# Hybrid pooling and short-convolution block, fp32 on one core: plain transfers issued by SP instead of GpSimd, joins spread over ticks, and eight more Strassen steps

## The chip, the core and the metric

The kernel runs on one core of a Trainium2 chip. Times are device microseconds. Before the change the median of 3 runs is 2392.21 us (2391.22 to 2397.08).

A core has a matrix engine (PE, with weight loads shown as PEld), VectorE (DVE), ScalarE (ACT) and GpSimd (POOL). SP computes nothing and issues transfers. POOL issues transfers too, among its own work; those that add to what stands at the destination (called gathers or joins here) are all POOL's.

## The reference

For 256 tokens of 4096 channels, all float32:

```python
h = rmsnorm(x, norm_w)
u_p, z_p, u_c, b_c, c_c, z_c, g_logit = split(h @ w_in)   # four times 2048 and two, then 2 * 4096 columns
y_pool = causal_multiscale_pool(u_p, pool_w, pool_scale) * silu(z_p)
y_conv = b_c * (conv_b + causal width-3 convolution of (c_c * u_c)) * silu(z_c)
br = einsum('bsnc,ncd->bsnd', stack([y_pool, y_conv]), w_branch)
gates = sigmoid(g_logit + gate_b)
x = x + sum(gates * br, over n) @ w_out
return rmsnorm(x, final_norm_w)
```

The pooling averages each channel group over a trailing window of 2, 4, 8 or 16 tokens, subtracts the token and applies a 512 x 512 map for each group. The weights, some 580 MB, are read once.

## The kernel before, in words

**Products.** Every float32 operand is split into a high part rounded to fp32r and the low rest, and a product is three matmuls (high x high, high x low, low x high) of 128 x 128 by 128 x 512. The work is cut into *units* of 1024 output columns and each unit into *steps* of 256 input channels (16 steps for w_in and w_out, 8 for w_branch). A step of kind P multiplies plainly: 24 matmuls. A step of kind S is a Strassen step: 7 products, 21 matmuls, for which DVE and ACT form sums of weight quarters first. The strings at the top (`SIX5`, `NINE`, `TEN`, ...) give a unit's steps in order. B and M steps in `HOST` are the pooling's band and map products.

**Order of units.** cz0, cb0, cu0, cc0, the same four with 1, then pz0, pu0, pz1, pu1 (pooling), g0_0, g0_1, g1_1, g0_2, g1_2, g0_3, g1_3, g1_0 (gates), b0_0, b1_0, ... b1_3 (branch products), o0 to o3 (output). I call them the c, p, g, branch and out stages; z, u, b, c in a name say which projection it is.

**A step's way.** SP loads the weights of a step (1 MB) into one of four `raw` slots (`issue_load`). For an S step this is two loads, 256 KB and 768 KB, and POOL then gathers another 256 KB quarter onto the first (`gather` in `issue_load`). ACT rounds the high parts into cells of `ring` (27 cells), DVE writes the low parts and, for S, the sums (`parts`). A slot is free for the load four steps on when its step is prepared. PE then multiplies from `ring` with the standing operand in `arena`. `pump` issues loads and preparation as far as slots and cells allow, up to four steps ahead.

**End of a unit.** PE's banks are copied by ACT: plain sums to E or Y (`evacuate`), the Strassen corners to J, and DVE adds the corners up (`corner_sums`). `combine` joins J to E or Y: for a unit marked `late` by two POOL transfers that add J to it in memory (512 KB each), otherwise on DVE. Then the unit's *epilogue*, a list of small actions, runs beside the next unit. One entry of the list is taken at each *tick*, every 6 matmuls of PE in the program (`TICK`), and `gap(n)` is n empty entries. What is left at a unit's end is flushed at once. In the last unit, o3, whose last three steps run separately, the list is already flushed after step 7 of the 13 before those.

**Epilogues that matter here.** In g units: `rescale` by the first norm's factor on ACT, then `bias` (two POOL transfers that add a row of gate_b, broadcast to all partitions, 512 KB each), the sigmoid, and a store to `gates_d`. In out units: `row` (two POOL transfers that add the residual rows of x to E), `start` (loads the final norm's weight row, broadcast, into Y[:, 0]), two squares on ACT, DVE's product `mul(E, E, Y[:, 0:1] ...)`, and a store to `o_d`. In c units the gate product is parked in `g_d` and results go to `y_d`.

**Fills.** The operands of the branch and out stages are read back from `y_d` and `m_d` into one of three stages (sa, sb, sc), summed and written into `arena` (`Fill`, `pop_fill`), one action a tick. After a late unit no new fill is fetched for `HUSH` ticks.

**Side operand.** A unit of nine or ten S steps runs one or two of the plain operands as Strassen operands too; the four formed sums of one of them lie in the tile `side`. After the first S step of a TEN unit those of the other are loaded (`side_load`, 512 KB, POOL).

**Queues.** Each engine executes in program order. `load` is SP's, `feed` ACT's; `move` (line 83) and `gather` (line 86) are POOL's. So every plain store and reload, every gather of a weight quarter, every join, row and bias stands in one queue, POOL's. An instruction that waits there holds up all behind it.

Of the kernel before, what the change touches and what calls it, by code (L numbers as in the profile page):

```python
# [15 lines left out]
P = 128  # L16
T = 256
D = 4096
HALF = D // 2
# [20 lines left out]
NINE_A = "PSPSSPSPSSPSPSPS"  # L40
NINE_P = "PSPSSPSPSSPSSPSP"
HOST = "PPBPPMMPSSPSSPSSPSS"
# [9 lines left out]
def hybrid_block(ctx: ExitStack, tc: tile.TileContext, x, xc, prm, rows_in, w_in, pool_w, w_branch, w_out, out):  # L52
# [28 lines left out]

    def move(dst, src):
        return pin(nc.gpsimd.dma_start(dst, src))

# [456 lines left out]
    def side_load(i):  # L541
        move(side["tile"], side_d[i - ND + 2])

    def side_items(i):
        def scaled():
# [6 lines left out]
            lambda: sub(side["tile"][:, 1], sa[:, 0:4], side["tile"][:, 0].bitcast(F32)),  # L552
            lambda: move(side_d[i - ND + 2], side["tile"])]

    def silu_y(late):
        def silu(t):
            act(Y[:, t], Y[:, t], AF.Silu, **(dict(scale=rin[:, t:t + 1]) if late else {}))
        return gap(18 if late else 3) + [lambda: silu(0), None, lambda: silu(1)]

    def rescale(d):  # L560
        return gap(18) + [lambda: act(d[:, 0], d[:, 0], scale=rin[:, 0:1]), None,
                          lambda: act(d[:, 1], d[:, 1], scale=rin[:, 1:2])]

    def conv_units(c, first):
        base = 2 * HALF + c * NU

        def b_epi(u):
            def product(t):
                stt(E[:, t], E[:, t], rin[:, t:t + 1], Y[:, t], ALU.mult, ALU.mult)
            return gap(18) + [lambda: product(0), None, lambda: product(1), None, lambda: move(g_d[c], E)]  # L570

        def c_epi(u):
# [21 lines left out]
            for j, n in enumerate((1, 7, 8, 8)):  # L594
                items += gap(n) + [lambda j=j: taps(j)]
            return items + [None, lambda: mul(chan(E), chan(J), chan(Y)), lambda: put(y_d[1, c], chan(E))]

        u = in_unit(f"cz{c}", base + 3 * HALF, lambda u: silu_y(u.late) + (gap(4) + side_items(ND - 1) + side_items(ND - 2) if first else []),
                    FIRST if first else SIX5, dst=Y)
        u.late = not first  # L600
        in_unit(f"cb{c}", base + HALF, b_epi, TEN if c else NINE_A).late = True
        u = in_unit(f"cu{c}", base, lambda u: rescale(Y), NINE, dst=Y)
        u.late = True
        in_unit(f"cc{c}", base + 2 * HALF, c_epi, NINE_A).urgent = lambda: mul(E, E, Y)

    def pool_units(c):
        u = in_unit(f"pz{c}", HALF + c * NU, lambda u: silu_y(True) + gap(4) + band_items(c), HOST if c else SIX5, dst=Y)
        u.late = True
        in_unit(f"pu{c}", c * NU, lambda u: [], NINE_P).urgent = lambda: None

# [70 lines left out]
    def mix(st):  # L681
# [14 lines left out]
        if g == 1:  # L696
            c = st.c

            def copy(j):
                for i in range(2):  # L700
                    b = 2 * j + i
                    act(chan(E)[:, b], bankview(j)[:, i], scale=scale_col(8 * c + b))
            queue.extend(gap(3) + transposes(Y, copy) + [lambda: put(y_d[0, c], chan(E))])

    def gate_unit(n, c):
        first, final = (n, c) == (0, 0), (n, c) == (1, 0)

        def epi(u):
# [18 lines left out]
    def branch_unit(n, c):  # L727
        def epi(u):
            if n == 0:
                if c:  # L730
                    return gap(10) + [lambda: move(spare(), gates_d[1, c])] + gap(8) + [lambda: mul(Y, E, Y)]
                return gap(8) + [lambda: mul(Y, E, Y)]
# [15 lines left out]
            return gap(2) + [gated, None, lambda: add(E, E, Y), None,  # L748
                lambda: c < 3 and move(Y, gates_d[0, c + 1])] + gap(4) + pairs(transposes(E, copy)) + [stored]

# [9 lines left out]
    def out_unit(c):  # L760
# [5 lines left out]
        def epi(u):  # L766
# [57 lines left out]
    now, quiet, hush = [0], [0], [0]  # L824
    LANDING, STORED, QUIET, HUSH = 12, 7, 5, 14

# [74 lines left out]
    def fetch_rows(c):  # L901
        (move if c else load)(E, xrows[:, :, c * NU:(c + 1) * NU])

# [213 lines left out]
    for u in units:  # L1117
# [149 lines left out]
```

## Time and profile before

| | |
|---|---|
| median of 3 runs | 2392.21 us (2391.22 to 2397.08) |
| the profiled execution | 2399.75 us |
| its span | 2398.0 us |
| mean granted PE clock | 0.994 |
| PE busy | 2355.6 us, 98% |
| DVE busy | 2085.4 us, 87% |
| ACT busy | 1496.9 us, 62% |
| POOL busy | 328.0 us, 14% |
| moved from and to memory | 627.71 MB, mean 262 GB/s |

The profile is of one execution, 7.5 us longer than the median of the runs. A row of the timeline reads: start, duration, engine, line, operation, out<-in, shape, count, and in brackets how long the engine had been idle and what ended that. Busy time of single matmuls overlaps (each lasts about 0.39 us and the next starts earlier), so a step's time is taken from starts. `raw<-in_w_in_dram` on SPq is a weight load, the same on POOL the gather of a quarter; `E<-J` is a join; `E<-in_rows_dram` a bias row; `E<-in_x_dram` a residual row; `Y<-in_rows_dram` from `start` the final norm's row.

### The profile page before, as it was taken

Reading aid. Unit: us, or ns where it says so; the run is one execution under the profiler, and the core shown is the slowest. Engines: PE = TensorE matmul, PEld = TensorE weight load, DVE = VectorE, ACT = ScalarE, POOL = GpSimd, SP = SyncE. Lnnn points to the kernel's source line nnn. Section 1 sums busy time; section 2 is a strip of 40 time slices with the busy share of each in tenths; the row PEclk is TensorE's granted clock in tenths of the full one; section 3 lists DMA queues with packets and bytes.
Section 4 is the critical chain, followed back from the end, with each engine's and each line's share of the span. In section 5 each row is a group of like instructions: output and inputs, shape, how many; then the busy total and the mean of one; then the engine's idle time right before and its main releaser. Section 6 shows DMA issues by size and latency. Waiting matters only on the chain.

```text
span 2398.0 us, 28884 instructions
## 1 busy us (share of the span) xinstructions
PE 2355.6 (98%) x10424; PEld 1940.0 (81%) x10424; DVE 2085.4 (87%) x2034; ACT 1496.9 (62%) x1590; POOL 328.0 (14%) x417
## 2 busy tenths in 40 slices
PE   9999999999999999999999999999999999999997
PEld 7888888888888888888787778888888888887776
DVE  8789988989879979979889889888898889889878
ACT  6565656656665656656666666676656557556555
POOL 0011100111001111111112111112101111111110
PEclk9999999999999999999999999999999999999999
DMA  9789877988868768768999899999879788888997
GB/s 372 235 263 269 255 236 229 274 256 250 263 229 253 233 214 259 233 216 249 262 286 271 266 291 273 282 292 289 272 234 296 239 294 281 258 251 249 273 264 261
DMA packets 159328, 627.71 MB, mean 262 GB/s; under 512 B 17424, under 2 KB 17680, under 8 KB 127184
## 3 DMA queue, kind: packets, MB, share of 16 engines
q1 hardware_dynamic: 101792, 485.40, 56.0%
q0 software_dynamic: 56816, 139.22, 28.4%
q8 instruction: 81, 1.33, 0.2%
q10 hardware_dynamic: 576, 1.24, 0.1%
q14 instruction: 63, 0.52, 0.1%
HBM read 579.66 MB, written 25.17 MB: 252 GB/s over the span
## 4 chain that ended last, share of the span: by engine, by line
PE 78%; DMA 8%; DVE 7%; issue 4%; ACT 2%; POOL 1%; SPq 0%; DVEq 0%; ACTq 0%; POOLq 0%
PE sums L1045 57%; PE shared L1045 19%; DMA raw<-in_w_in_dram 6%; DVE ring L62 4%; DMA raw<-in_w_out_dram 2%; DVE parts L62 2%; ACT ring L59 2%; PE shared L690 1%; PE shared L476 1%; POOL E L86 1%; ACT J L59 0%; ACT E L59 0%; DVE J L62 0%; PE shared L666 0%; PE shared L667 0%
## 5 line engine op out<-in xcount | busy, mean ns | idle before, releaser
L1045 PE MATMUL sums<-ring,arena 128*128 128x512 f32 x7011 | 1649.4, 391 | 27.1 <-DVE ring L62 23.3
L1045 PEld LDWEIGHTS sums<-ring,arena 128*128 128x128 f32 x7011 | 1313.4, 188 | 309.7 <-DVE ring L62 34.3
L62 DVE TENSOR_TENSOR ring<-raw,ring 128x512 fp32r<-128x512 f32 (+3 forms) x904 | 1086.2, 1220 | 133.3 <-ACT ring L59 57.0
L59 ACT ACTIVATE ring<-raw 128x1024 fp32r<-128x1024 f32 (+3 forms) x661 | 882.3, 1370 | 321.8 <-DMA raw<-in_w_in_dram 98.4
L59 ACT ACTIVATE ring<-parts 128x1024 fp32r<-128x1024 f32 (+1 forms) x451 | 372.5, 840 | 415.5 <-DVE parts L62 307.4
L1045 PE MATMUL shared<-ring,arena 128*128 128x512 f32 x2241 | 545.9, 392 | 0.0
L1045 PEld LDWEIGHTS shared<-ring,arena 128*128 128x128 f32 x2241 | 424.4, 189 | 89.5
L62 DVE TENSOR_TENSOR ring<-parts,ring 128x1536 fp32r<-128x1536 f32 (+2 forms) x258 | 391.8, 1530 | 14.6 <-ACT ring L59 14.6
L86 POOL DMA_DIRECT2D raw<-in_w_in_dram x168 | 145.3, 865 | 1332.3 <-DMA raw<-in_w_in_dram 597.4
L62 DVE TENSOR_TENSOR parts<-raw,parts 128x1024 f32<-128x1024 f32 x222 | 270.5, 1219 | 0.0
L62 DVE TENSOR_TENSOR parts<-raw 128x512 f32<-128x512 f32 x222 | 152.4, 687 | 61.6 <-DMA raw<-in_w_out_dram 28.3
L62 DVE TENSOR_TENSOR J<-J 128x512 f32<-128x512 f32 (+1 forms) x90 | 78.3, 870 | 39.2 <-ACT J L59 36.7
L1045 PE MATMUL sums<-ring,last_pair 128*128 128x512 f32 x306 | 78.0, 392 | 3.1 <-DVE ring L62 3.1
L59 ACT ACTIVATE J<-shared 128x512 f32<-128x512 f32 x128 | 68.4, 627 | 11.4 <-PE shared L476 10.7
L1045 PEld LDWEIGHTS sums<-ring,last_pair 128*128 128x128 f32 x306 | 57.0, 188 | 17.3 <-DVE ring L62 5.6
L59 ACT ACTIVATE E<-sums 128x512 f32<-128x512 f32 x76 | 41.8, 599 | 32.9 <-PE sums L1045 31.8
L86 POOL DMA_DIRECT2D raw<-in_w_out_dram x31 | 27.7, 893 | 219.1 <-DVE ring L62 97.4
L86 POOL DMA_DIRECT2D raw<-in_w_branch_dram x23 | 20.2, 877 | 245.7 <-DMA raw<-in_w_branch_dram 86.5
L1045 PE MATMUL shared<-ring,last_pair 128*128 128x512 f32 x216 | 52.0, 390 | 0.0
L1045 PE MATMUL shared<-ring,side 128*128 128x512 f32 x207 | 50.7, 389 | 0.0
L1045 PEld LDWEIGHTS shared<-ring,last_pair 128*128 128x128 f32 x216 | 40.5, 188 | 8.6
L1045 PEld LDWEIGHTS shared<-ring,side 128*128 128x128 f32 x207 | 38.9, 188 | 8.1
(142 smaller groups left out, 718.6 us busy)
## 6 DMA issues: line engine op xcount, KB each, us to landing
raw<-in_w_in_dram SPq DMA_DIRECT2D x150, 1024.0 KB, 7.0
raw<-in_w_in_dram SPq DMA_DIRECT2D x168, 768.0 KB, 6.8
raw<-in_w_in_dram SPq DMA_DIRECT2D x176, 256.0 KB, 5.9
raw<-in_w_in_dram POOLq DMA_DIRECT2D x168, 256.0 KB, 6.0
raw<-in_w_branch_dram SPq DMA_DIRECT2D x41, 1024.0 KB, 7.3
raw<-in_w_out_dram SPq DMA_DIRECT2D x33, 1024.0 KB, 7.3
raw<-in_w_out_dram SPq DMA_DIRECT2D x31, 768.0 KB, 6.5
raw<-in_w_branch_dram SPq DMA_DIRECT2D x23, 768.0 KB, 5.5
```

Source lines behind the costliest of these rows:

```text
L59: return pin(nc.scalar.activation(dst, src, func, **kw))
L62: return pin(nc.vector.tensor_tensor(out=dst, in0=a, in1=b, op=op))
L86: return pin(nc.gpsimd.dma_start(dst, src, accum_op=ALU.add))
L476: pin(nc.tensor.transpose(shared(j)[:, i * T + t * P:i * T + (t + 1) * P], src[:, t, c:c + P], ident))
L690: pin(nc.tensor.matmul(o, a, b, start=(k, i) == (0, 0), stop=(k, i) == (3, 2)))
L1045: pin(nc.tensor.matmul(ps, lhs, rhs, start=n == 0, stop=n == u.total[b] - 1))
```

## The change

`move` now issues on SP, and the old one on POOL stays as `aside` for the side operand and the first rows of x. The two joins of a late unit become entries 5 and 8 of the epilogue list instead of being issued at its start; the lists behind them are shortened (18 to 12 empty entries), the two biases and the two residual rows are set three entries apart, and the rows of out units come 8 entries after the joins. Stores get four or five empty entries ahead of them. `HUSH` goes from 14 to 20. cu, cc and pu take ten S steps instead of nine (`TEN`, `TEN_P`), cz1 and pz0 seven instead of six (`SEVEN5`), and each new TEN unit brings a side load.

```diff
-NINE_P = "PSPSSPSPSSPSSPSP"
+TEN_P = "PSPSSPSSPSSPSSSP"
+SEVEN5 = "PPPPPSPSPSPSSPSS"
...
     def move(dst, src):
+        return pin(nc.sync.dma_start(dst, src))
+
+    def aside(dst, src):
         return pin(nc.gpsimd.dma_start(dst, src))
...
             if u.late:
-                for t in range(2):
-                    gather(d4[:, t], q[:, t])
+                for t, n in ((0, 4), (1, 2)):
+                    queue.extend(gap(n) + [lambda t=t: gather(d4[:, t], q[:, t])])
...
     def rescale(d):
-        return gap(18) + [lambda: act(d[:, 0], d[:, 0], scale=rin[:, 0:1]), None,
+        return gap(12) + [lambda: act(d[:, 0], d[:, 0], scale=rin[:, 0:1]), None,
...
-                    FIRST if first else SIX5, dst=Y)
+                    FIRST if first else SEVEN5, dst=Y)
...
-        u = in_unit(f"cu{c}", base, lambda u: rescale(Y), NINE, dst=Y)
+        u = in_unit(f"cu{c}", base, lambda u: rescale(Y), TEN, dst=Y)
         u.late = True
-        in_unit(f"cc{c}", base + 2 * HALF, c_epi, NINE_A).urgent = lambda: mul(E, E, Y)
+        in_unit(f"cc{c}", base + 2 * HALF, c_epi, TEN).urgent = lambda: mul(E, E, Y)
...
-        in_unit(f"pu{c}", c * NU, lambda u: [], NINE_P).urgent = lambda: None
+        in_unit(f"pu{c}", c * NU, lambda u: [], TEN_P).urgent = lambda: None
...
-            items = (rescale(d) if u.late else gap(1)) + [lambda: bias(0), lambda: bias(1)] + gap(12) + [
+            items = (rescale(d) if u.late else gap(1)) + [lambda: bias(0), None, None, lambda: bias(1)] + gap(12) + [
                 lambda: gate(0), None, lambda: gate(1)]
-            return items if first or final else items + [lambda: move(gates_d[n, c], E)]
+            return items if first or final else items + gap(5) + [lambda: move(gates_d[n, c], E)]
...
-            return gap(2) + [lambda: row(0), lambda: row(1)] + gap(12) + [start] + gap(8) + [
+            return gap(8) + [lambda: row(0), None, None, lambda: row(1)] + gap(12) + [start] + gap(6) + [
                 lambda: square(0), lambda: square(1),
-                lambda: mul(E, E, Y[:, 0:1].to_broadcast([P, 2, NU])), lambda: move(o_d[c], E)]
+                lambda: mul(E, E, Y[:, 0:1].to_broadcast([P, 2, NU]))] + gap(5) + [lambda: move(o_d[c], E)]
...
-    LANDING, STORED, QUIET, HUSH = 12, 7, 5, 14
+    LANDING, STORED, QUIET, HUSH = 12, 7, 5, 20
...
-            if u.text is TEN and st.kind == "S" and st.op in x_ops[:ND] and st is not u.steps[-1]:
+            if u.text in (TEN, TEN_P) and st is next(q for q in u.main if q.kind == "S"):
                 side_load(2 * ND - 3 - x_ops.index(st.op))
```

Three places of the program, before and after. In the rows, what stands in brackets are the semaphores an instruction waits for: DMASW of POOL's transfers, DMAHW of SP's, the others of engines.

The first is POOL at the end of o0. Before:

```order
L86 DMA raw<-in_w_out_dram 128x512 [waits DMAHW1_49,DMASW7_49,DVE_49]
L86 DMA E<-J 128x2x512 [waits DMASW0_49,DVE_49,Activation_49]
L86 DMA E<-J 128x2x512 [waits DMASW1_49,Activation_49]
L86 DMA E<-in_x_dram 128x1024 [waits DMASW2_49,DMASW0_49]
L86 DMA E<-in_x_dram 128x1024 [waits DMASW3_49,DMASW1_49]
L86 DMA raw<-in_w_out_dram 128x512 [waits DMAHW4_49,DMASW4_49,DVE_49]
L86 DMA raw<-in_w_out_dram 128x512 [waits DMAHW0_49,DMAHW6_49,DMASW5_49,DVE_49]
L83 DMA sa<-m_d 128x512 [waits DMASW6_49]
L83 DMA Y<-in_rows_dram 128x1024 [waits DMASW7_49]
```

And POOL at the same place after the change:

```order
L90 DMA raw<-in_w_out_dram 128x512 [waits DMAHW3_49,DMASW3_49,DVE_49]
L90 DMA E<-J 128x2x512 [waits DMASW4_49,DVE_49,Activation_49]
L90 DMA raw<-in_w_out_dram 128x512 [waits DMAHW6_49,DMASW5_49,DVE_49]
L90 DMA E<-J 128x2x512 [waits DMASW6_49,PE_49]
L90 DMA raw<-in_w_out_dram 128x512 [waits DMAHW0_49,DMAHW2_49,DMASW7_49,DVE_49]
L90 DMA E<-in_x_dram 128x1024 [waits DMASW4_49,DMASW0_49]
L90 DMA raw<-in_w_out_dram 128x512 [waits DMAHW3_49,DMAHW5_49,DMASW1_49,DVE_49]
L90 DMA E<-in_x_dram 128x1024 [waits DMASW6_49,DMASW2_49]
```

Each residual row still waits for its join, but a weight gather now stands between any two of the four, and fill and final row have left the queue.

The second is the flush in o3. Before, POOL holds the final row (of o2's epilogue), two weight gathers, the store and the next final row:

```order
L86 DMA raw<-in_w_out_dram 128x512 [waits DMAHW1_49,DMASW4_49,DVE_49]
L83 DMA Y<-in_rows_dram 128x1024 [waits DMASW5_49]
L86 DMA raw<-in_w_out_dram 128x512 [waits DMAHW4_49,DMASW6_49,DVE_49]
L86 DMA raw<-in_w_out_dram 128x512 [waits DMAHW6_49,DMAHW0_49,DVE_49]
L83 DMA o_d<-E 128x2048 [waits DMASW2_49,DMASW1_49,DVE_49]
```

After the change SP holds them among the weight loads:

```order
L78 DMA raw<-in_w_out_dram 128x512 [waits DMAHW7_49,DMAHW5_49,DVE_49]
L78 DMA raw<-in_w_out_dram 128x1536
L84 DMA Y<-in_rows_dram 128x1024
L84 DMA o_d<-E 128x2048 [waits DMASW3_49,DMASW6_49,DMASW2_49,DMAHW0_49,DMASW0_49,DVE_49]
L84 DMA Y<-in_rows_dram 128x1024 [waits DMAHW7_49,DMAHW1_49]
L78 DMA raw<-in_w_out_dram 128x2048 [waits DMASW1_49,DMAHW2_49,DVE_49,Activation_49]
```

The final row, the store that needs it through DVE's product, and the next final row now follow each other without a step between.

The third is DVE at the last fill of o0 (arena<-sa). Before:

```order
L62 TENSOR_TENSOR ring<-raw,ring 128x1536
L62 TENSOR_TENSOR ring<-parts,ring 128x1536 [waits PE_49,Activation_49]
L62 TENSOR_TENSOR arena<-sa,arena 128x896
L62 TENSOR_TENSOR ring<-raw,ring 128x1024 [waits DMAHW2_49,PE_49,Activation_49]
L62 TENSOR_TENSOR ring<-raw,ring 128x1024 [waits PE_49,Activation_49]
L62 TENSOR_TENSOR parts<-raw 128x512 [waits DMAHW4_49,DMASW5_49,DVE_49]
```

After:

```order
L63 TENSOR_TENSOR ring<-parts,ring 128x1536 [waits PE_49,Activation_49]
L63 TENSOR_TENSOR ring<-raw,ring 128x1024 [waits DMAHW4_49,PE_49,Activation_49]
L63 TENSOR_TENSOR ring<-raw,ring 128x1024 [waits PE_49,Activation_49]
L63 TENSOR_TENSOR arena<-sa,arena 128x896 [waits Activation_49]
L63 TENSOR_TENSOR parts<-raw 128x512 [waits DMAHW6_49,DMASW1_49,DVE_49]
```

The fill has moved behind the two instructions that prepare a P step.

More of the change, by code (lines that the diff above doesn't have):

```diff
@@ L541, in side_load @@
     def side_load(i):
-        move(side["tile"], side_d[i - ND + 2])
+        aside(side["tile"], side_d[i - ND + 2])
     def side_items(i):
@@ L552, in side_items @@
             lambda: sub(side["tile"][:, 1], sa[:, 0:4], side["tile"][:, 0].bitcast(F32)),
-            lambda: move(side_d[i - ND + 2], side["tile"])]
+            None, None, None, None, lambda: aside(side_d[i - ND + 2], side["tile"])]
     def silu_y(late):
@@ L569, in product @@
                 stt(E[:, t], E[:, t], rin[:, t:t + 1], Y[:, t], ALU.mult, ALU.mult)
-            return gap(18) + [lambda: product(0), None, lambda: product(1), None, lambda: move(g_d[c], E)]
+            return gap(12) + [lambda: product(0), None, lambda: product(1)] + gap(5) + [lambda: move(g_d[c], E)]
         def c_epi(u):
@@ L702, in copy @@
                     act(chan(E)[:, b], bankview(j)[:, i], scale=scale_col(8 * c + b))
[L703 removed]
+            queue.extend(gap(3) + transposes(Y, copy) + gap(5) + [lambda: put(y_d[0, c], chan(E))])
     def gate_unit(n, c):
@@ L730, in epi @@
                 if c:
-                    return gap(10) + [lambda: move(spare(), gates_d[1, c])] + gap(8) + [lambda: mul(Y, E, Y)]
+                    return gap(4) + [lambda: move(spare(), gates_d[1, c])] + gap(8) + [lambda: mul(Y, E, Y)]
                 return gap(8) + [lambda: mul(Y, E, Y)]
@@ L748, in epi @@
             return gap(2) + [gated, None, lambda: add(E, E, Y), None,
-                lambda: c < 3 and move(Y, gates_d[0, c + 1])] + gap(4) + pairs(transposes(E, copy)) + [stored]
+                lambda: c < 3 and move(Y, gates_d[0, c + 1])] + gap(4) + pairs(transposes(E, copy)) + gap(4) + [stored]
         text = (B1 if c else B1_FIRST) if n else B0_MORE if c else B0
@@ L901, in fetch_rows @@
     def fetch_rows(c):
-        (move if c else load)(E, xrows[:, :, c * NU:(c + 1) * NU])
+        (aside if c else load)(E, xrows[:, :, c * NU:(c + 1) * NU])
     def square(c):
```

7 lines of the change are left out of this document (4 added, 3 removed).

## The prediction

> **What bounds the kernel now.** I read the page first, then busy time by stretch, then the waits of PE and the places in its timeline where it stood idle, and last the queues and engines that PE waited for there.
>
> ```profile
> span 2398.0 us, 28884 instructions
> PE 2355.6 (98%) x10424; PEld 1940.0 (81%) x10424; DVE 2085.4 (87%) x2034; ACT 1496.9 (62%) x1590; POOL 328.0 (14%) x417
> 2185.40 7.48 PE sums L1045 x33
> ```
>
> PE is the bound: it is idle for 2398.0 - 2355.6 = 42.4 us in all. Where it runs without a break, the chain of waits gives 33 matmuls in 7.48 us, 0.2267 us each. So a change can gain in two ways only: fewer matmuls, or less of those 42.4 us (and of the time that PE ran at a lower clock). The next rows say where they lie.
>
> ```profile
> core 0: us, PE busy (x) PEld busy (x) DVE busy (x) ACT busy (x) POOL busy (x), PEclk, DMA share, GB/s
> 400.00:500.00 100.00, 100.00 (x442) 82.61 (x441) 93.26 (x89) 64.60 (x64) 14.08 (x16) 1.00 0.87 266
> 1118.00:1201.00 83.00, 80.44 (x352) 65.31 (x351) 73.01 (x67) 55.26 (x57) 13.42 (x15) 1.00 0.93 266
> 1430.90:1434.20 3.30, 3.30 (x10) 2.53 (x9) 3.27 (x5) 1.09 (x3) 0.00 (x0) 0.50 1.01 397
> 2161.50:2168.10 6.60, 4.57 (x11) 3.62 (x12) 6.57 (x10) 6.18 (x9) 0.00 (x0) 0.50 0.69 213
> 2250.10:2256.80 6.70, 5.40 (x13) 4.24 (x14) 6.67 (x6) 6.46 (x9) 0.00 (x0) 0.50 0.69 218
> 2338.90:2342.20 3.30, 3.01 (x7) 2.44 (x8) 3.30 (x4) 3.27 (x5) 0.85 (x1) 0.50 0.58 209
> ```
>
> The first stretch, 400 to 500 us, is the end of cz1 and most of cb1, a unit of ten S steps: PE has no idle time there. A g unit (1118 to 1201) loses 2.6 us. The last four rows are the short stretches in which the granted clock was 0.50: each follows an idle stretch of PE.
>
> ```profile
> PE sums L1045 <- DVE ring L62: 10.3, 10, 2.5
> 1178.95 1.45 PE L1045 MATMUL sums<-ring,arena 128*128 128x512 f32 x5 [1.87 <-DVE ring L62]
> 1429.73 1.60 PE L1045 MATMUL sums<-ring,arena 128*128 128x512 f32 x5 [2.48 <-DVE ring L62]
> 1729.48 1.42 PE L1045 MATMUL sums<-ring,arena 128*128 128x512 f32 x5 [1.61 <-DVE ring L62]
> 1740.67 12.53 PE L1045 MATMUL sums<-ring,arena 128*128 128x512 f32 x54 [0.92 <-ACT E L59]
> 2160.00 0.50 PE L1045 MATMUL sums<-ring,arena 128*128 128x512 f32 x1 [1.31 <-ACT ring L59]
> 2163.53 2.50 PE L1045 MATMUL sums<-ring,arena 128*128 128x512 f32 x5 [3.03 <-DVE ring L62]
> 2175.82 6.87 PE L1045 MATMUL sums<-ring,arena 128*128 128x512 f32 x29 [0.31 <-DVE ring L62]
> 2247.88 0.49 PE L1045 MATMUL sums<-ring,arena 128*128 128x512 f32 x1 [0.43 <-ACT ring L59]
> 2251.40 2.50 PE L1045 MATMUL sums<-ring,arena 128*128 128x512 f32 x5 [3.03 <-DVE ring L62]
> 2339.19 2.50 PE L1045 MATMUL sums<-ring,arena 128*128 128x512 f32 x5 [3.87 <-DVE ring L62]
> ```
>
> The first row sums the g stage (window 1100 to 1610): 10.3 us in 10 waits. Then two of those, the two at the start of the branch stage, and the six of the out stage: one group in each of o1, o2 and o3. Idle time plus half of the busy time at clock 0.50 is what a place cost: g stage 10.3 + 1.65 = 12.0; o1 1.31 + 3.03 + 0.31 + 2.3 = 6.9; o2 0.43 + 3.03 + 2.7 = 6.2; o3 3.87 + 1.5 = 5.4; branch stage 1.61 + 0.92 = 2.5. That is 33.0 us in the reach of this change. The rest of the idle time is the opening and the tail.
>
> The clock: 2.48 us of idle were followed by clock 0.50, 1.87 us were not. [...]
>
> What PE waits for in the out stage is one queue:
>
> ```profile
> 2128.15 2.66 POOL L86 DMA_DIRECT2D E<-J  x2
> 2139.47 0.90 POOL L86 DMA_DIRECT2D E<-in_x_dram  x1 [8.66 <-DMA E<-J]
> 2145.16 0.86 POOL L86 DMA_DIRECT2D E<-in_x_dram  x1 [4.79 <-DMA E<-J]
> 2145.86 1.09 POOL L86 DMA_DIRECT2D raw<-in_w_out_dram  x1
> 2157.95 0.69 DVE L62 TENSOR_TENSOR parts<-raw 128x512 f32<-128x512 f32 x1 [9.49 <-DMA raw<-in_w_out_dram]
> 2335.03 0.69 DVE L62 TENSOR_TENSOR parts<-raw 128x512 f32<-128x512 f32 x1 [10.17 <-DMA raw<-in_w_out_dram]
> ```
>
> After o0, POOL issues both joins, then stands 8.66 + 4.79 us with the residual rows, which add to the same E, until each join has landed. The weight gather of the next Strassen step is queued behind them. DVE then idles 9.49 us and PE 4.65. In o3 DVE idles 10.17 and PE 3.87: PE has about 6.3 us of prepared work as cover, and what goes beyond it is lost.
>
> **The change part by part.**
>
> *Strassen steps.* Eight steps change from P (24 matmuls) to S (21): two each in cu, cc and pu, one in cz1, one in pz0. That removes 8 x 3 x 0.2267 = 5.4 us of PE.
>
> ```profile
> 2140.15 0.69 DVE L62 TENSOR_TENSOR parts<-raw 128x512 f32<-128x512 f32 x1
> 2145.83 1.22 DVE L62 TENSOR_TENSOR ring<-raw,ring 128x1024 fp32r<-128x1024 f32 x1
> 2116.13 1.09 DVE L62 TENSOR_TENSOR arena<-sa,arena 128x896 fp32r<-128x896 f32 x1
> 2117.14 2.35 DVE L62 TENSOR_TENSOR ring<-raw,ring 128x1024 fp32r<-128x1024 f32 x2
> 2117.73 1.52 PE L1045 MATMUL sums<-ring,arena 128*128 128x512 f32 x6
> ```
>
> DVE prepares an S step from 2140.15 to 2145.83, 5.7 us, and a P step in about 2.3. So a unit of 81 us gets 3.4 us more DVE work, plus a 256 KB gather and, for six units, a side load of 512 KB. DVE stands at 93.26 of 100 us with PE full in the first stretch above, so there is room, but little. A new TEN unit costs between nothing (that stretch) and the 2.6 us of the g unit; the g unit has bias rows and a store besides, so I take 0.33 each, 2 us for six, with 0 to 10 as bounds.
>
> *Joins and residual rows of o1 and o2.* The joins go to ticks 5 and 8, the rows to 17 and 20; a tick is 6 matmuls, 1.36 us. Between join and row lie 12 ticks, 16 us.
>
> ```profile
> E<-J POOLq DMA_DIRECT2D x6, 512.0 KB, 13.9
> E<-in_x_dram POOLq DMA_DIRECT2D x6, 512.0 KB, 9.5
> Y<-in_rows_dram POOLq DMA_DIRECT2D x4, 512.0 KB, 11.5
> raw<-in_w_out_dram SPq DMA_DIRECT2D x23, 1024.0 KB, 7.4
> ```
>
> A join lands 13.9 us after issue, so POOL's wait shrinks from 13.5 us to a few at most, under the cover, and weight gathers now stand between the pieces. I take the whole 6.9 + 6.2 = 13.1. If the second join starts late, behind a gather that waits for its own load, some waiting comes back: the low bound is 5.
>
> *o3.* Here the items are flushed after seven of its steps, at tick 26. Before, the row of the final weights (Y<-in_rows) was issued at tick 17, ahead of that. Now its place is tick 33, so the flush issues it itself, on SP, and DVE's product E<-E,Y stands right behind the preparation that frees the slot SP waits for. DVE thus waits out the whole landing. The trace has none of these on SP: 7.4 us (the nearest SP load) and 11.5 (the same transfer from POOL) bound it; I take 8.5, nearer SP's. With the product itself,
>
> ```profile
> 2342.99 2.29 DVE L62 TENSOR_TENSOR E<-E,Y 128x2048 f32<-128x2048 f32 x1
> ```
>
> PE's stall is 8.5 + 2.2 - 6.3 = 4.4 us, and some 2 at half clock, 6.4 against 5.4 now: a loss of 1.0. With o1's cover, 9.49 - 4.65 = 4.8, it would be 1.5 more. Ends: a gain of 5.4 if the cover is longer, a loss of 6 at a landing of 11.5.
>
> *The last operand of o0.* HUSH holds the operand fills back by six more ticks after a unit with late joins. The last fill of o0 (arena<-sa) ended at about 2117.2, 0.5 us before PE read it at 2117.73. Now it stands behind the next P preparation, 2.3 us: a stall of 1.8. Bounds 0 and 4.
>
> *g stage.* The gates go out by SP, the bias rows are three ticks apart, the joins too. POOL's queue is shorter, but the bytes are the same. I take half of the 12.0, 6, with 0 and 12 as bounds.
>
> ```profile
> q1 hardware_dynamic: 101792, 485.40, 56.0%
> q0 software_dynamic: 56816, 139.22, 28.4%
> ```
>
> By these rows a MB takes 0.20% of the engines' time from POOL and 0.12% from SP, so 1 MB less on POOL in each g unit is worth 0.08% of 2398 us, 2 us of transfer time per unit whose DMA share is 0.93: some relief. [...]
>
> *Branch stage.* The bias of g1_0 gets two ticks more before its sigmoid, and fills leave POOL: 1 of 2.5 us (0 to 2.5).
>
> *All other plain moves* cost nothing by my sum: stores stand four to five ticks behind the DVE or ACT work they wait for, so SP finds it done. What is queued behind such a store is the next weight load, and DVE waits for that; the cover is the 6.3 us above. In the branch stage SP can also stand at a fill until the store that it reads back has landed:
>
> ```profile
> m_d<-last_pair POOLq DMA_DIRECT2D x6, 512.0 KB, 5.9
> ```
>
> Seven ticks, 9.5 us, lie between, so that is hidden too, or 2 us within the cover if SP issues the store late.
>
> Sum: 5.4 + 13.1 - 1.0 - 1.8 + 6 + 1 - 2 = 20.7 us less. The profiled execution took 2399.75 us (span 2398.0), so it would take 2379; the median of the runs is 7.5 lower, 2392.2, and the sum taken from it gives 2371.5.
>
> **The rivals.**
>
> *All these waits vanish* (chance 0.12). For it: spreading removes the cause in every stage. Against: the DMA share of 0.93. 5.4 + 13.1 + 12 + 2.5 = 33 less, 2359.
>
> *The transfers bound it, so spreading moves the waits only* (0.15). For: the same bytes move in the same units, at a DMA share of 0.93. g and branch stages gain nothing, o1 and o2 half: 5.4 + 6.5 - 1.0 - 1.8 - 2 = 7 less, 2385, on the edge of what can be told. [...]
>
> *SP's queue becomes the choke* (0.09). Weight loads now stand behind moves that wait for their data. If SP stands at the gate store of each g unit longer than the 6.3 us of cover, each of these six units pays what o1 paid, 6.9 instead of 2.0: 29 more, and without the 6 and the 1 the rest gives 13.7 less, so 2392 + 16 = 2408. It ends slower from about 4.3 us lost per g unit. Against: the stores' own gaps.
>
> **How the numbers follow.** My forecast has 0.64. About 0.3% (7 us) is what a measurement of this kernel can tell. Under 2385: the forecast, the first rival and a third of the second, 0.81. Within 0.3%: the rest of the second, 0.10. Slower: 0.09. The range runs from 2357, just past the first rival, to 2388, past the second; with the bounds of the g stage, o1 and o2 it leaves out the last rival and odd ends.
>
> **What would show it.** Right: PE with 10400 matmuls; no PE wait over 1 us at the start of o1 and o2, and POOL's waits for E<-J under 5 us; a PE wait of 3 to 5 us in o3 behind a DVE wait for Y<-in_rows; one near 2 us in the last step of o0; g waits near 5 us in all; cu, cc and pu with less than 0.5 us idle each. Wrong: new PE waits in c, u or pu units, g waits as before, or SP standing at a store.

## The result, and the profile after

The changed kernel takes 2415.56 us, median of 6 runs (2404.85 to 2421.70), against 2392.72 us for the kernel before (6 runs beside it, 2389.89 to 2397.08). The ratio is 1.008 with a 95% interval of [1.0056, 1.0104]: 19 us slower by the ratio (22.8 by the medians), where 20.7 us faster was forecast. In this and every later comparison, each kernel is set against runs of the kernel before taken beside it, and microseconds are the ratio's distance from 1 times 2394 us. An interval is some 3 to 6 us to each side, so the difference between two edited kernels is uncertain by some 5 to 9 us. Two executions with a mean clock of 0.849 and 0.242 (2602.94 us of the kernel before, 9344.17 us of e12_early) count in no ratio.

The profiled execution is the fastest of the six: 2404.85 us, span 2403.1. The kernel before was profiled in an execution 7.5 us above its median, so the two traces lie only 5.1 us apart; they show where time went, not how much of the 19 us each place took. Its page, with the line of the chain by engine from both pages (before, then after):

```profile
PE 78%; DMA 8%; DVE 7%; issue 4%; ACT 2%; POOL 1%; SPq 0%; DVEq 0%; ACTq 0%; POOLq 0%
```

```profile
span 2403.1 us, 28906 instructions
PE 2351.3 (98%) x10400; PEld 1933.4 (80%) x10400; DVE 2112.0 (88%) x2061; ACT 1509.8 (63%) x1592; POOL 297.5 (12%) x356
PE 66%; DMA 16%; DVE 10%; issue 4%; ACT 3%; POOL 0%; SPq 0%; DVEq 0%; ACTq 0%; POOLq 0%
```

The 24 matmuls are gone, and PE is busy 4.3 us less. But it is idle 2403.1 - 2351.3 = 51.8 us, 9.4 more than before, and more of the end's chain runs through transfers. Roughly by stage (cut at 20, 655, 1085, 1632, 2050 and 2362 us in both traces), from the idle times of all of PE's rows, with the time at clock 0.50 below:

| | opening | c | p | g | branch | out | tail |
|---|---|---|---|---|---|---|---|
| idle before, us | 4.0 | 0.5 | 1.6 | 10.4 | 2.9 | 12.0 | 11.1 |
| idle after | 2.1 | 6.6 | 4.8 | 11.8 | 2.9 | 12.3 | 11.4 |
| half clock before | 0 | 0 | 0 | 3.4 | 0 | 17.1 | 10.1 |
| half clock after | 0 | 0 | 0 | 0 | 0 | 13.7 | 9.5 |

So the c and p stages lose 9 us that they did not lose before, and the g and out stages, which were to gain 16 us, gain almost nothing. The waits of the changed kernel say who is late (engine, what it works on, what it waited for; sum, times, longest):

```profile
PE sums L1049 <- DVE ring L63: 26.0, 21, 8.6
ACT E L60 <- DMA gates_d<-E: 20.0, 4, 5.8
ACT Y L60 <- DMA Y<-J: 17.2, 6, 4.2
DVE E L63 <- DMA Y<-in_rows_dram: 12.7, 1, 12.7
PE sums L1049 <- ACT E L60: 9.8, 6, 2.7
ACT E L60 <- DMA E<-J: 9.7, 5, 2.2
ACT E L60 <- DMA o_d<-E: 6.3, 1, 6.3
```

For the kernel before, the same view has no wait of ACT for a store or a join. When ACT writes E and Y it waits mostly for PE, and PE behind it hardly at all (the two largest rows, and PE's):

```profile
ACT E L59 <- PE sums L1045: 44.0, 20, 3.3
ACT Y L59 <- PE sums L1045: 19.2, 7, 5.5
PE sums L1045 <- ACT E L59: 0.9, 1, 0.9
```

Three kinds of wait are new: ACT copying PE's banks into E while the previous unit's store still reads E, ACT rescaling a result whose join has not landed, and DVE in o3 waiting for the norm's row. The end of one g unit shows the first two. These rows of the timeline, of ACT, SP, ACT and PE, are the list of g1_2 beside g0_3 and g0_3's first copied bank:

```profile
1485.38 1.16 ACT L60 ACTIVATE E<-E,rin 128x1024 f32<-128x1024 f32 x1 [1.93 <-DMA E<-J]
1523.30 0.37 SPq L84 DMA_DIRECT2D gates_d<-E  x1
1533.94 0.60 ACT L60 ACTIVATE E<-sums 128x512 f32<-128x512 f32 x1 [5.76 <-DMA gates_d<-E]
1536.87 3.31 PE L1049 MATMUL sums<-ring,arena 128*128 128x512 f32 x12 [1.75 <-ACT E L60]
```

The store is issued at 1523.30 and lands 10.6 us later; g0_3 is at its last step by then, and ACT stands 5.76 us before it may overwrite E. In the kernel before, this store goes out at 1510.35, and ACT's copy at 1526.85 has waited only for PE:

```profile
1510.35 0.83 POOL L83 DMA_DIRECT2D gates_d<-E  x1
1526.85 0.60 ACT L59 ACTIVATE E<-sums 128x512 f32<-128x512 f32 x1 [3.27 <-PE sums L1045]
```

The joins of g1_2 went out at 1468.59 and 1471.13 us in the changed kernel, behind a weight gather of POOL's that had stood 12.57 us for its own load; in the kernel before both went out from 1455.60 on. The second landed 14.2 us after its issue, and the rescale at 1485.38 had to wait for it.

The places in the out stage, rows of PE in the changed kernel, and then the row of DVE that o3 waits for:

```profile
2127.26 1.88 PE L1049 MATMUL sums<-ring,arena 128*128 128x512 f32 x7 [0.99 <-DVE arena L63]
2161.62 7.64 PE L1049 MATMUL sums<-ring,arena 128*128 128x512 f32 x33
2296.58 3.69 PE L1049 MATMUL sums<-ring,arena 128*128 128x512 f32 x8 [2.71 <-ACT E L60]
2353.59 2.50 PE L1049 MATMUL sums<-ring,arena 128*128 128x512 f32 x5 [8.58 <-DVE ring L63]
2347.23 2.29 DVE L63 TENSOR_TENSOR E<-E,Y 128x2048 f32<-128x2048 f32 x1 [12.68 <-DMA Y<-in_rows_dram]
```

The last fill of o0 costs 0.99 us; the second row runs through the matmul of o1 ahead of which 3.03 us stood before; between o2 and o3 is a new wait, for the store of o1's result (o_d<-E); and o3 waits 8.58 us, not 3.87.

Most of the 11 us by which the median lies above this execution is the clock: its mean granted clock is 0.996, that of the other five 0.992 to 0.994, and 0.996 on the mean for 31 runs of the kernel before. 0.003 of 2400 us is 7 us.

### The profile page after: what moved, and what is told of

Read it like the earlier page. It is cut to its first block, busy times and chain, and to the rows that moved or that the text cites. A ratio compares the mean times of both kernels' runs of the same rounds, so it can differ in the third digit from the quotient of the medians.

```text
span 2403.1 us, 28906 instructions
## 1 busy us (share of the span) xinstructions
PE 2351.3 (98%) x10400; PEld 1933.4 (80%) x10400; DVE 2112.0 (88%) x2061; ACT 1509.8 (63%) x1592; POOL 297.5 (12%) x356
## 4 chain that ended last, share of the span: by engine, by line
PE 66%; DMA 16%; DVE 10%; issue 4%; ACT 3%; POOL 0%; SPq 0%; DVEq 0%; ACTq 0%; POOLq 0%
PE sums L1049 48%; PE shared L1049 16%; DMA raw<-in_w_in_dram 12%; DVE ring L63 7%; DVE parts L63 2%; DMA Y<-J 2%; ACT ring L60 2%; DMA gates_d<-E 2%; PE shared L694 1%; PE shared L480 1%; DVE J L63 1%; ACT J L60 1%; DMA Y<-in_rows_dram 0%; DMA o_d<-E 0%; ACT E L60 0%
## 5 line engine op out<-in xcount | busy, mean ns | idle before, releaser
L1049 PE MATMUL sums<-ring,arena 128*128 128x512 f32 x6873 | 1622.8, 391 | 36.3 <-DVE ring L63 24.6
L1049 PEld LDWEIGHTS sums<-ring,arena 128*128 128x128 f32 x6873 | 1288.0, 188 | 318.2 <-DVE ring L63 36.5
L63 DVE TENSOR_TENSOR ring<-raw,ring 128x1024 fp32r<-128x1024 f32 (+3 forms) x907 | 1085.6, 1217 | 133.1 <-ACT ring L60 72.7
L60 ACT ACTIVATE ring<-parts 128x1024 fp32r<-128x1024 f32 (+1 forms) x464 | 385.1, 844 | 408.8 <-DVE parts L63 328.1
L1049 PE MATMUL shared<-ring,arena 128*128 128x512 f32 x2283 | 554.1, 390 | 1.5 <-DVE ring L63 1.5
L63 DVE TENSOR_TENSOR ring<-parts,ring 128x1536 fp32r<-128x1536 f32 (+2 forms) x268 | 406.1, 1527 | 37.9 <-ACT ring L60 27.7
L90 POOL DMA_DIRECT2D raw<-in_w_in_dram x176 | 152.2, 865 | 1388.8 <-DMA raw<-in_w_in_dram 678.2
L63 DVE TENSOR_TENSOR parts<-raw,parts 128x1024 f32<-128x1024 f32 x230 | 280.6, 1220 | 0.0
L63 DVE TENSOR_TENSOR parts<-raw 128x512 f32<-128x512 f32 x230 | 158.2, 688 | 18.1 <-issue 13.1
L60 ACT ACTIVATE J<-shared 128x512 f32<-128x512 f32 x128 | 68.3, 623 | 11.4 <-PE shared L480 10.7
L1049 PE MATMUL shared<-ring,side 128*128 128x512 f32 x261 | 63.9, 389 | 0.0
L1049 PEld LDWEIGHTS shared<-ring,side 128*128 128x128 f32 x261 | 49.0, 188 | 10.2
```

Source lines behind the costliest of these rows:

```text
L60: return pin(nc.scalar.activation(dst, src, func, **kw))
L63: return pin(nc.vector.tensor_tensor(out=dst, in0=a, in1=b, op=op))
L90: return pin(nc.gpsimd.dma_start(dst, src, accum_op=ALU.add))
L1049: pin(nc.tensor.matmul(ps, lhs, rhs, start=n == 0, stop=n == u.total[b] - 1))
```

## The experiments

I tested three theories. *Steps*: the new Strassen steps cost DVE more than they save PE. *Late*: the lists were spread so far that stores, joins and the norm's row come after those who need them, or need what they hold. *Queue*: the third rival, SP's queue holds up weight loads. In the edits the names are those of the code.

**1. The strings alone** (e1_texts): the kernel before with the new strings and the side load's condition.

```diff
-NINE_P = "PSPSSPSPSSPSSPSP"
+TEN_P = "PSPSSPSSPSSPSSSP"
+SEVEN5 = "PPPPPSPSPSSPSPSS"
...
-        u = in_unit(f"cu{c}", base, lambda u: rescale(Y), NINE, dst=Y)
+        u = in_unit(f"cu{c}", base, lambda u: rescale(Y), TEN, dst=Y)
...
```

`SEVEN5` stands here as the kernel has it; in the diff ahead of the prediction its eleventh and twelfth step are exchanged.

> The kernel before with the eight added Strassen steps alone (strings and side load of the changed kernel; queues and lists as before). Theory 'steps' (the added steps cost DVE and transfers more than the 24 matmuls save; PE idle in the c and p stages rose from 2.1 to 11.1 us): 3 to 10 us slower than the kernel before, c and p idle near 11 us. Theory 'late' (what was spread or delayed now arrives after those who need it) and theory 'queue' (SP's queue holds up weight loads): 2 to 5 us faster, c and p idle under 4 us.

Ratio 1.0044 [1.0026, 1.0062], 10.5 us slower; c and p idle 10.5 us. *Steps* has its number, at the upper end. Eight steps that save 5.4 us of PE cost 16 us gross, 10.5 and the 5.4 saved.

**2. All but the strings** (e2_old_texts): the same edit backwards, on the changed kernel.

> The changed kernel with the old strings: no added Strassen steps, all of the spreading and SP's queue kept. 'steps': 3 to 10 us faster than the changed kernel, so 10 to 18 us slower than before, c and p idle back to 2 us. 'late' and 'queue': 0 to 6 us slower than the changed kernel, so 20 to 28 us slower than before; c stage waits of over 1 us stay.

1.0068 [1.0042, 1.0095], 16.3 us slower than before and 2.9 less than the changed kernel, between what *steps* and the other two expected. So the strings are not the whole: queues and lists alone lose 16 us. c and p are idle 7.3 us, more than *steps* allows.

**3. POOL as issuer** (e3_pool): in `move`, `nc.sync` becomes `nc.gpsimd`.

> The changed kernel with all plain moves issued by POOL again; spreading and strings stay as changed. 'queue': 12 us or more faster than the changed kernel, no more than 8 us slower than before. 'late': within 6 us of the changed kernel, since a store stands at the same tick whoever issues it; ACT still waits for gates_d<-E and o_d<-E near the end of units, and DVE in o3 for Y<-in_rows_dram.

1.0047 [1.0027, 1.0067], 11.3 us slower, 7.9 less than the changed kernel: neither the 12 that *queue* asked for nor the 6 that *late* allowed, and hardly clear of the noise. ACT's waits for gates_d<-E are 15.1 us here, for Y<-J 19.6, and o3's wait is 10.11. Most of the lateness stays whoever issues.

**4. Stores at once** (e4_stores): the stores (g_d, y_d, gates_d, m_d, o_d) back directly behind the work that they wait for; two of the lines are shown.

```diff
-            return items if first or final else items + gap(5) + [lambda: move(gates_d[n, c], E)]
+            return items if first or final else items + [lambda: move(gates_d[n, c], E)]
...
-                lambda: mul(E, E, Y[:, 0:1].to_broadcast([P, 2, NU]))] + gap(5) + [lambda: move(o_d[c], E)]
+                lambda: mul(E, E, Y[:, 0:1].to_broadcast([P, 2, NU])), lambda: move(o_d[c], E)]
```

> The changed kernel with the stores (g_d, y_d, gates_d, m_d, o_d) at once behind the work they wait for, as before, instead of four to five ticks later; all else as changed. 'late': ACT's waits for gates_d<-E (20.0 us in the g stage) and o_d<-E (6.3 us) go; PE's waits <-ACT E (9.8 us and 1.7 us of half clock) go with them: 8 to 15 us faster than the changed kernel. 'queue': SP stands at the stores for DVE and ACT, weight loads come later: same or up to 15 us slower than the changed kernel.

1.0048 [1.0031, 1.0065], 11.5 us slower, 7.7 less than the changed kernel, just short of the 8 to 15 expected. The waits of this kernel that answer:

```profile
ACT Y L60 <- DMA Y<-J: 18.0, 6, 4.8
DVE E L63 <- DMA Y<-in_rows_dram: 11.8, 1, 11.8
ACT E L60 <- DMA E<-J: 9.7, 5, 2.2
PE sums L1049 <- ACT E L60: 3.1, 1, 3.1
```

No wait for gates_d<-E or o_d<-E is left; those for joins and the norm's row stand as they were. g is idle 3.2 us instead of 11.8: the relief that the prediction sought there exists, the late store had eaten it. The other traces agree: g is idle 2.5 to 5.7 us in the seven with its stores at once and its list spread, 7.3 to 11.5 in the five with the old list, and 10.2 to 16.2 in the five with late stores.

**5. Old strings and stores at once** (e5_old_now): 2 and 4 together.

> The changed kernel with the old strings and with the stores at once behind their work: what stays is SP as issuer, the spread joins, rows and bias, and HUSH 20. 'late' alone (the rest of the loss is o3's 7 to 8 us of PE idle and some 3 us more of half clock than before, against 13 us gained at o1 and o2): within 6 us of the kernel before. 'queue': 8 us or more slower than before, with DVE waits for weights behind SP's stores. If the two parts taken out overlap little, their sum (some 5 us for the strings, 11 us for the stores) gives 2 to 6 us slower than before.

1.0007 [0.9994, 1.0019]: 1.7 us slower, which is what *late* said and not what *queue* said. From e2_old_texts to this, the stores alone are worth 14.6 us, well clear of the noise.

**6. The out units' list earlier** (e6_o3), on the changed kernel:

```diff
-                for t, n in ((0, 4), (1, 2)):
+                for t, n in ((0, 1), (1, 2)) if u.name[0] == "o" else ((0, 4), (1, 2)):
...
-            return gap(8) + [lambda: row(0), None, None, lambda: row(1)] + gap(12) + [start] + gap(6) + [
+            return [start] + gap(8) + [lambda: row(0), None, None, lambda: row(1)] + gap(9) + [
```

> The changed kernel with the out units' list earlier: joins at ticks 1 and 4, start (Y<-in_rows_dram) ahead of the rows, rows some 7 ticks sooner. If o3's wait is for the late start, as the trace says (DVE 12.7 us, PE 8.6 us and 10.2 us at half clock): the PE wait in o3 falls to under 4 us and the time by 7 to 12 us against the changed kernel. If the transfers bound it and the wait only moves (to the rows or to o2's first steps): under 3 us faster, with a new wait of 4 us or more in o1, o2 or o3.

1.0053 [1.0031, 1.0075], 6.5 us less than the changed kernel, a little under the 7 to 12 expected and by itself not clear of the noise. In o3 PE now waits twice, 1.49 and 1.94 us, without loss of clock:

```profile
2345.16 1.43 PE L1049 MATMUL sums<-ring,arena 128*128 128x512 f32 x5 [1.49 <-DVE ring L63]
2357.60 1.43 PE L1049 MATMUL sums<-ring,arena 128*128 128x512 f32 x5 [1.94 <-DVE ring L63]
```

The wait for Y<-in_rows_dram is gone and PE's wait in o3 is under 4 us, so the late start was o3's cause. The waits of o1 and o2 do not grow to match: the out stage is idle 7.3 us instead of 12.3.

**7. 5 and 6 together** (e7_best_sp): old strings, stores at once, start early, SP as issuer.

> e5_old_now with the out units' list of e6_o3: old strings, stores at once, spread joins, start early, SP as issuer. 'late': o1, o2 and o3 lose under 4 us together, the g stage under 6 us: 5 to 15 us faster than the kernel before. 'queue': no faster than before.

0.9975 [0.9959, 0.9992], 6.0 us faster than before. g is idle 5.7 us, the out stage 6.7, more than the 4 expected, but with no half clock outside the tail.

**8. The out units alone** (e8_out): the kernel before, POOL as issuer, with the out units' joins at ticks 1 and 4 and the list of 6.

> The kernel before with the out units alone changed: joins at ticks 1 and 4, start first, rows at ticks 14 and 17; all issued by POOL, strings as before. Term B of the prediction (the boundary waits of o1 and o2 cost 13 us and vanish when spread) with o3's 5.4 us partly: 11 to 18 us faster than before, PE waits at the starts of o1 and o2 under 1 us. 'transfers bound, waits only move': 0 to 7 us faster, new waits inside o1, o2 or o3.

0.9989 [0.9974, 1.0005]: 2.6 us faster (not clear of 0), not 11 to 18, so under POOL "waits only move" has its number. PE waits 2.92 us in o1 and 3.71 in o3, each with 6.8 us at half clock. Rows of POOL and PE after o0:

```profile
2126.57 2.66 POOL L86 DMA_DIRECT2D E<-J  x2
2128.02 1.81 POOL L83 DMA_DIRECT2D Y<-in_rows_dram  x1
2143.48 0.87 POOL L86 DMA_DIRECT2D raw<-in_w_out_dram  x1 [13.65 <-DMA raw<-in_w_out_dram]
2165.95 2.50 PE L1048 MATMUL sums<-ring,arena 128*128 128x512 f32 x5 [2.92 <-DVE ring L62]
```

Ticks 1 and 4 did not part the two joins, since nothing stood between them in POOL's queue; the gather behind these three transfers waits 13.65 us for its own load.

**9. DVE's part of the new steps alone** (e9_dve): the kernel before, strings as before; one P step in each of the eight units also runs, into `parts`,

```python
sub(parts[:, 0], q[:, 3], q[:, 1])
sub(parts[:, 1:3], q[:, 0:3:2], parts[:, 0:1].to_broadcast([P, 2, NH]))
sub(parts, q[:, 0:3], parts)
```

> The kernel before, strings unchanged, with only the DVE work of an S step added to one P step in each of the eight units (0.69 + 1.22 + 1.75 us into a buffer that P steps don't use; no fewer matmuls, no gather, no side load, no ring cells). 'DVE' (the added steps cost what they cost because DVE has no time left there): e1_texts was 10.3 us slower in spite of 5.4 us of PE saved, so this one is 10 to 18 us slower than before, with new PE waits in cu, cc and pu. 'Transfers or ring cells' (the extra gather, side load or look-ahead are the cost): within 4 us of before.

1.0050 [1.0031, 1.0069], 12.0 us slower, with no other part of a Strassen step. DVE is busy 2113.0 us, as with the strings (2112.0). So added DVE work is enough to lose as much. But that the strings lose their time in the same way is not shown. Much of the loss stands at one place of this trace, in pu0, where DVE also builds the pooling's masks (PE waited 1.05 us there before; rows of PE, DVE and POOL):

```profile
810.53 2.50 PE L1053 MATMUL sums<-ring,arena 128*128 128x512 f32 x5 [6.33 <-DVE ring L62]
807.24 0.28 DVE L643 TENSOR_REDUCE cnt<-sa 128x1 f32<-128x128 f32 x1 [3.33 <-POOL sa L631]
805.40 0.88 POOL L86 DMA_DIRECT2D raw<-in_w_in_dram  x1 [8.03 <-DMA raw<-in_w_in_dram]
```

DVE itself stands idle there, for masks that POOL makes only after a weight gather that waited 8.03 us for its own load, and 6.8 us at half clock follow. In e1_texts DVE waits 0.55 us at this point and PE nowhere more than 2.50 us in the c and p stages.

**10. Strings without the new side loads** (e10_no_side).

> e1_texts without the six new side loads of cu, cc and pu (512 KB each; their S steps multiply the other operand's sums, so part of the result is left out). 'DVE': like e1_texts, 7 to 12 us slower than before. 'Transfers': at least 5 us of e1_texts' 10.3 us come back, 0 to 5 us slower than before.

1.0030 [1.0012, 1.0047], 7.2 us slower: at the edge of what 'DVE' allows. The side loads are worth some 3 us by these two ratios, but the intervals of this and e1_texts overlap, so their share stays open.

**11. Issuer, once nothing is late** (e11_best_pool): e7_best_sp with `move` on POOL.

> e7_best_sp with the plain moves issued by POOL. 'queue' (SP as issuer costs): at least 5 us faster than e7_best_sp, 13 us or more faster than before. If the issuer matters little once nothing is late: within 4 us of e7_best_sp. If POOL's queue was the choke that the prediction took it for: 4 to 10 us slower than e7_best_sp.

0.9968 [0.9951, 0.9984], 1.7 us less than e7_best_sp: the issuer makes no difference that can be told here, so neither *queue* nor POOL's queue as the choke.

**12. Joins earlier too** (e12_early): e7_best_sp with all joins at ticks 1 and 4, `gap(12)` ahead of rescale, silu and product made `gap(16)`, so that these stay where they were.

> e7_best_sp with the joins of all late units at ticks 1 and 4 instead of 5 and 8, and what needs them at the same ticks as before. 'late' (ACT and DVE waits for Y<-J and E<-J in the c and p stages are lateness too; e7_best_sp has two PE waits of 1.8 us there): 3 to 6 us faster than e7_best_sp. If those waits have another cause: within 2 us.

0.9943 [0.9921, 0.9965], 13.6 us faster than before, 7.6 better than e7_best_sp: the best of all, a little more than expected. What is left of the waits above:

```profile
PE sums L1048 <- DVE ring L62: 13.8, 15, 2.1
PE sums L1048 <- ACT E L59: 1.3, 2, 0.7
```

```profile
span 2378.5 us, 28853 instructions
PE 2350.1 (99%) x10424; PEld 1938.9 (82%) x10424; DVE 2085.5 (88%) x2034; ACT 1500.2 (63%) x1590; POOL 283.8 (12%) x342
```

PE's wait for DVE is half of what it was in either kernel, and no wait of ACT for a join or a store is listed.

**13. The strings in the best version** (e13_early_texts): 12 with the new strings.

> e12_early with the new strings: the whole change with nothing left that comes later than it must (joins at ticks 1 and 4, stores at once, start first in the out units). If the cost of the strings adds to the rest (DVE has no time left in cu, cc and pu whatever the queues do): 8 to 12 us slower than e12_early, within 5 us of the kernel before. If the strings cost only because other things were late beside them: within 4 us of e12_early or faster, 9 us or more faster than before.

0.9960 [0.9945, 0.9975], 9.6 us faster than before, 4 us slower than e12_early, some 9 gross. Added to other kernels the strings cost 10.5 us (the kernel before), 2.9 (e2_old_texts) and 9.8 (from e5_old_now to e4_stores). These four differ by no more than the noise, so whether the strings cost less once nothing is late is not settled. It is also the whole change with its lateness taken out: the same steps, issuer and HUSH, 29 us faster than as it was made.

**14. HUSH** (e14_hush): 20 back to 14 in e12_early.

> e12_early with HUSH at 14 as before instead of 20. The prediction's term for the last fill of o0 was 1.8 us; the changed kernel's trace has 0.99 us there and e12_early's has none over 0.2 us. So within 3 us of e12_early. If the later fills have a price that the trace of one execution does not show (fills beside the next unit's start, or the reverse, quiet bought by the longer pause): 4 us or more from e12_early in either direction.

0.9947 [0.9931, 0.9964]: no difference from e12_early that can be told.

**15. The joins alone** (e15_joins): the joins and gaps of 12 on the changed kernel.

> The changed kernel with the joins alone earlier: ticks 1 and 4 instead of 5 and 8, what needs them at the same ticks as before; late stores, start, strings kept. Taken from e7_best_sp to e12_early the same edit gave 5 us. 'Late': 3 to 8 us faster than the changed kernel, so 12 to 18 us slower than before, with ACT's waits for E<-J and Y<-J (21 us in the c, p and g stages) nearly gone. If the edit paid only where the stores were at once: within 2 us of the changed kernel, 19 us or more slower than before.

1.0040 [1.0023, 1.0057], 9.6 us less than the changed kernel, as much as it gave in 12 or more. No wait for E<-J or Y<-J is left, while the one for the stores has grown, in an execution 5 us above this kernel's median, from 20.0 to 26.6 us:

```profile
ACT E L60 <- DMA gates_d<-E: 26.6, 4, 7.8
PE sums L1049 <- ACT E L60: 21.7, 8, 3.9
PE sums L1049 <- DVE ring L63: 16.6, 15, 4.1
```

Put in a row, each kernel is the one above with one edit. The step of the stores is well clear of the noise, those of the joins and of the out units' list barely, the last one not:

| kernel | edit | against before, us |
|---|---|---|
| e12_early | spread, all early, old strings | -13.6 |
| e7_best_sp | joins to ticks 5 and 8 | -6.0 |
| e5_old_now | out units' list late, start behind the rows | +1.7 |
| e2_old_texts | stores 4 to 5 ticks later | +16.3 |
| the changed kernel | new strings | +19.2 |

## Why the prediction was wrong

**The step that failed** is "All other plain moves cost nothing by my sum: stores stand four to five ticks behind the DVE or ACT work they wait for, so SP finds it done." It asked what a store waits for, and not who waits for the store. The next unit's evacuation writes the same E. The stores' delay was put at 0 and is worth 14.6 us by the ladder (7.7 with the strings in). Of the same kind, and left out of the sum: the joins, moved later while rescale, silu and the product came at nearly the same ticks, 7.6 to 9.6 us. Their landing of 13.9 us stood in the prediction, but was used only for the rows behind them, and so was its warning of a join behind a gather that waits for its own load.

Without the new strings (5.4 gained, 2 paid) the sum forecast 17.3 us less. The spreading with nothing late, e12_early, gave 13.6 less. So the total was near for the change that the prediction had in mind; what the sum missed is the lateness, and the strings' price. The prediction's own signs of being wrong, new PE waits in c and u units and g waits as before, both stand in the trace.

**Strassen steps.** PE's 5.4 us came (10400 matmuls). The cost of the new TEN units was taken as 2 us with 10 as bound; it measured 16 gross alone and 9 to 10 in the best version. The price came from one unit in which PE had no idle time with DVE at 93%; that showed room for that unit's work, not for 3.4 us more of it. By the traces, c and p together are idle 6.7 to 15.1 us in the eight with the new strings and 2.1 to 7.3 in the eight with the old ones (10.3 in e9_dve). The windows of 480 to 560 us, the end of cb1 and the greater part of cu1, before and after, are one example:

```profile
480.00:560.00 80.00, 79.68 (x352) 65.40 (x350) 71.39 (x66) 48.29 (x50) 10.77 (x12) 1.00 0.85 261
```

```profile
480.00:560.00 80.00, 77.96 (x344) 64.23 (x344) 74.85 (x73) 49.47 (x53) 11.70 (x13) 1.00 0.88 263
```

DVE goes from 71.39 to 74.85 of 80 us, close to the 3.4 us expected, and PE's idle time from 0.32 to 2.04. But e9_dve has DVE busy 74.81 us in the same window and PE idle for 0.26 only, and e12_early, with the old strings, has PE idle for 2.52. That the strings cost more than they save is shown in the kernel before; that DVE's time is the price is argued.

**o1 and o2.** Right as to the place: no PE wait at either start. But 13.1 us was too much to count on. It was read in an execution at clock 0.994, 7.5 us above the median, with 13.7 us of half clock at these two places; e1_texts, with the same list in its out units, has 3.4 there. Alone, under POOL, the edit gave 2.6 (e8_out), and in the change the border of o2 and o3 paid 2.71 us and 1.7 of clock to the store.

**o3.** The mechanism was the one predicted, to the row: DVE behind a wait for Y<-in_rows_dram, PE's cover 12.68 + 2.29 - 8.58 = 6.4 us (6.3 predicted). The mis-sized term is DVE's wait: 8.5 was taken for it and 12.68 came, a landing of 11.3, near the upper bound of 11.5, and 1.4 around its issue. With it came 10.2 us at half clock. o3 lost 13.7 us against 5.4 before, and not 6.4.

**g and branch stages.** -6 and -1 forecast, nothing came: the g stage lost 11.8 us, against 12.0. The relief was there (3.2 idle in e4_stores) and went to the late gate stores. But the reason given for it, a MB that costs more from POOL than from SP, does not hold: in the g stage the two queues took 92.1% of the engines' time before for 149.8 MB and 91.6% after for 150.1 MB, where 2 us for each of six units would have been 2.2%. **Last fill of o0:** 0.99 against 1.8, and HUSH has no price of its own.

**The rivals.** That all waits vanish came nearest in e12_early, without the steps. "The transfers bound it" falls: e12_early moves the same bytes as the kernel before in 13.6 us less. The third rival had the nearest time, 2408, but that was luck and not the cause: e5_old_now and e7_best_sp keep SP's queue and lose nothing by it, and in e12_early, the fastest, SP's plain moves stand 29.3 us behind DVE's E and 25.7 behind ACT's. In the changed kernel itself POOL as issuer gave 7.9 us back; the two intervals overlap a little, and why is not settled. Nor is it settled how much of the strings' cost is DVE's time, POOL's gathers or the side loads.

## What to carry to other kernels

When a store or a join is moved later, price it from its landing, not its issue (the gate store above landed 10.6 us after it, a join 14.2), and look up who next writes the buffer that it reads and who next reads the one that it fills; the cover is the time to that instruction, and here one delay of four to five ticks was worth 8 to 15 us. A full PE beside an engine at 93% does not show that the engine has room for more (the eight added steps cost 16 us gross), so measure the addition alone before trading it for matmuls. An execution several microseconds above the median can overstate terms that carry half clock (13.7 us of it at o1 and o2 in one 7.5 us above, 3.4 in e1_texts).

## What the runs showed of the hardware

The clock. In the prediction's rows 2.48 us of idle in g were followed by clock 0.50 and 1.87 us were not. In the changed kernel 2.46 us in b0_0 were not, and in e4_stores three gaps of 1.20, 0.22 and 0.52 us were. Two neighbouring windows of 3.4 us each, first of the changed kernel between o2 and o3, then in b0_0, then of e4_stores:

```profile
2293.24:2296.64 3.40, 0.69 (x4) 0.25 (x2) 0.57 (x1) 2.99 (x4) 0.86 (x1) 1.00 0.74 306
2296.65:2300.05 3.40, 3.40 (x8) 2.75 (x9) 1.81 (x3) 3.40 (x8) 0.00 (x0) 0.50 0.72 176
```

```profile
1743.68:1747.09 3.41, 2.52 (x12) 1.74 (x10) 3.34 (x3) 0.88 (x1) 0.00 (x0) 1.00 1.02 210
1747.10:1750.50 3.40, 1.84 (x8) 1.54 (x9) 3.37 (x8) 3.40 (x6) 0.86 (x1) 1.00 0.98 350
```

```profile
466.86:470.27 3.41, 1.50 (x5) 0.67 (x4) 1.93 (x3) 3.41 (x5) 0.00 (x0) 1.00 0.93 280
470.28:473.69 3.41, 3.38 (x8) 2.71 (x9) 3.41 (x5) 2.86 (x3) 0.00 (x0) 0.50 0.11 25
```

In the first and the third pair PE worked 0.69 and 1.50 us of a window, and the next ran at 0.50 (the clock stands third from the end). In b0_0 the 2.46 us lie in both windows, 0.90 and 1.56, and both ran at 1.00, as did the 3.40 us behind them, with 17 matmuls; the second window of the first pair, at 0.50, has 8. So in these traces the length of a single wait did not tell whether the clock fell: 2.48 us cost clock and 2.46 did not. What decides it was not shown. The clocks of 0.996 and 0.992 of the changed kernel's fastest and slowest runs would explain some 10 of the 17 us between them, an estimate from 0.004 of 2400 us; that the same waits cost clock in one execution and not in the other was argued here, not tried.
